# The output projection of a two-branch attention layer: eight block products, or seven with sums that DMAs make

## The chip, the cores and the metric

The kernel runs on one core of a Trainium2 chip. The metric is device time in microseconds, the median of several executions. TensorE (PE in the profile) multiplies, VectorE (DVE), ScalarE (ACT) and GpSimd (POOL) do the elementwise work, SyncE (SP) issues most DMAs. PSUM is the memory that TensorE writes to, SBUF the other on-chip memory.

## The reference

One layer on x of 1024 tokens by 1024, everything in float32:

```python
u = layer_norm(x) * (1 + scale) + shift          # scale, shift, gate = silu(c) @ w_ada + b_ada
fq, fk, fv, fg, ff, sq, sk, sv, sg = split(u @ w_in)
f_cum = cumsum(log_sigmoid(ff + b_f))
y_fox = softmax(causal(fq fk^T / 8 + f_cum_q - f_cum_k)) fv * silu(fg)     # 8 heads of 64
y_sb  = stick_breaking(sq, sk) sv * silu(sg)                               # 8 heads of 64
y = concat(y_fox, y_sb) @ w_out
out = layer_norm(2 ** 0.25 * x + gate * y, ln_g, ln_b)
```

The change is in the last two lines. Both are done tile by tile of 128 tokens.

## The kernel before

**Precision.** A float32 factor is split in a rounded part hi and a remainder lo, and a product is three TensorE products: hi·hi, lo·hi and hi·lo. One such group of three, 128 tokens by 128 of k by 512 columns, is called a step below.

**Stages.** The start makes scale, shift and the normalised u. Then the eight pairs of heads p = 0..7 follow (0 to 3 stick-breaking, 4 to 7 softmax). The attention of a pair is cut into 16 units (p, h, i): head h, block of 128 queries i. A unit has scores S on TensorE, softmax or stick-breaking on DVE, ScalarE and GpSimd, transposes T two units later, and for every two blocks a product with v ("pv"), from which `att_pv` makes a y piece of 64 x 256: ScalarE copy, DVE sum of the parts, GpSimd product with the gate branch (`sg`), and a DMA to the DRAM tensor `y_dr`. Between the units TensorE does "fillers": projections of the next pairs. In the last pair, from unit LAST + 4 on (LAST = 112 is its first), the fillers are steps of the output projection, in the numbers of TAIL: 68 steps before the loop ends, 60 after it.

**The order.** TensorE runs in the order in which the code is written, by hand (`manual_schedule`). The other engines get their order from a scheduler with modelled times. Every engine runs its own list in order: an instruction that waits holds all behind it.

**The output projection.** `gen_split_out`, beside the fillers of pairs 4 to 6, loads w_out in half blocks of 128 x 512, multiplies them by gate, and splits them on GpSimd into hi and lo, which go to DRAM (`wo_dr`). `load_wo` fetches them back in the last pair. `load_y` fetches y for a tile of 128 tokens and splits it on GpSimd. For pair 7, y does not go through DRAM: it stays in SBUF as `y7h` and `y7l`. `gen_out` makes 8 token tiles x 2 halves of 512 columns x 8 pairs = 128 steps, in the order of tiles 6, 7, 4, 5, 2, 3, 0, 1.

**The ending of a tile** (`o_half`, `ln_finish`), on DVE: 2^0.25 x + accumulator (L897), statistics (L899), aggregate (L170), GpSimd's two small operations for 1 / sqrt(var + eps) (L175, L176), two operations with gain (L910) and two with bias (L912), and the store. `lngb` is ln_g and ln_b in SBUF, for the first tiles; after the last unit `ln_to_psum` copies them to PSUM (`ps_gain`, `ps_bias`), and the rest use these.

## Time and profile before

| | |
|---|---|
| median of three runs | 684.96 us (684.79 to 685.23) |
| span of the profiled execution | 683.5 us |
| granted TensorE clock | 0.999 |
| TensorE busy | 667.2 us, 98% of the span, 4021 products recorded |
| VectorE, ScalarE, GpSimd busy | 450.6, 382.0, 427.7 us |
| first step of the output projection | 570.28 us |
| last pv product | 628.53 us |
| last TensorE product begins | 676.37 us |
| last store issued | 680.74 us |

The span runs from the first instruction to the last of the one profiled execution; the time of a run has 1.5 us more. A row of the timeline reads: start, duration, engine, line, operation, out<-in, shape, and in brackets the idle time before it and what ended it. A row of groups has its count, busy time and mean in ns at the end. Where a row says x2, its duration is that of two neighbours together. A few of TensorE's records are missing in a trace.

### The profile page before, as it was taken

The page shows a single profiled execution, that of the slowest core. Times are in us where ns is not written, and L with a number is a line of the kernel's source. Part 1 is how long each engine was busy: PE and PEld are TensorE (multiplying, and loading weights), DVE is VectorE, ACT ScalarE, POOL GpSimd, SP SyncE. Part 2 cuts the span into 40 slices and gives each one's busy share as a digit, 9 for nine tenths or more (in the row PEclk, how much of TensorE's full clock was granted, in tenths as well). Part 3 has the DMA queues.
Part 4 walks back from the last instruction along what each step waited for, and adds up shares of the span by engine and source line. Part 5 has one row for each costly group of instructions (what it writes and reads, how often), then busy time and mean ns, then how long its engine had stood idle before and what let it go on. Part 6 is the DMA issues. An engine that isn't in the chain of part 4 may idle for free.

```text
span 683.5 us, 11770 instructions
## 1 busy us (share of the span) xinstructions
PE 667.2 (98%) x4021; PEld 587.2 (86%) x4021; DVE 450.6 (66%) x914; ACT 382.0 (56%) x861; POOL 427.7 (63%) x558
## 2 busy tenths in 40 slices
PE   5999999999999999999999999999999999999995
PEld 4789898888998888889988888899988889888885
DVE  6785368867666667676675665765566677774645
ACT  5668357856567666566675564655565667531000
POOL 5558977756348566556388896877584364665411
PEclk9999999999999999999999999999999999999999
DMA  9966231112102121122144563453341298143301
GB/s 338 410 236 233 82 105 44 41 29 60 29 9 86 27 57 54 37 55 55 55 131 136 172 176 121 143 166 129 101 150 40 72 327 318 58 162 118 123 31 62
DMA packets 45036, 81.60 MB, mean 119 GB/s; under 512 B 5232, under 2 KB 18864, under 8 KB 44976
## 3 DMA queue, kind: packets, MB, share of 16 engines
q1 hardware_dynamic: 43536, 76.63, 33.8%
q10 hardware_dynamic: 1440, 4.21, 2.2%
q8 instruction: 32, 0.52, 0.3%
q14 instruction: 28, 0.23, 0.1%
HBM read 60.34 MB, written 16.29 MB: 112 GB/s over the span
## 4 chain that ended last, share of the span: by engine, by line
PE 94%; DMA 3%; DVE 2%; ACT 0%; issue 0%; POOL 0%; DVEq 0%
PE m L270 10%; PE m L272 10%; PE m L271 10%; PE pv L493 10%; PE T L478 9%; PE S L428 5%; PE S L427 5%; PE o L884 4%; PE o L882 4%; PE o L883 4%; PE v L327 4%; PE v L328 4%; PE v L329 4%; DMA raws<-in_w_qkg_dram 2%; PE st_late L589 1%; PE st_q L589 1%
## 5 line engine op out<-in xcount | busy, mean ns | idle before, releaser
L270 PE MATMUL m<-uh,whi 128*128 128x512 f32 x304 | 126.4, 416 | 0.0
L272 PE MATMUL m<-uh,wlo 128*128 128x512 f32 x304 | 119.7, 394 | 0.0
L271 PE MATMUL m<-ul,whi 128*128 128x512 f32 x304 | 119.7, 394 | 0.0
L481 DVE TENSOR_TENSOR pt<-T,pt 128x512 fp32r<-128x512 f32 (+2 forms) x192 | 100.5, 550 | 17.5 <-ACT pt L480 16.5
L461 POOL TENSOR_TENSOR be<-be,kp 128x127 f32<-128x127 f32 (+3 forms) x64 | 77.2, 1207 | 33.1 <-DVE kp L457 23.5
L480 ACT CAST pt<-T 128x512 fp32r<-128x512 f32 (+2 forms) x192 | 85.8, 480 | 16.1 <-PE T L478 12.5
L453 DVE TENSOR_TENSOR_SCAN kp<-kp,floor 128x512 f32<-128x512 f32 (+2 forms) x64 | 65.2, 1018 | 31.2 <-ACT kp L447 30.1
L493 PEld LDWEIGHTS pv<-pt,v 128*128 128x128 f32 (+1 forms) x640 | 77.1, 163 | 4.4 <-DVE pt L481 0.7
L493 PE MATMUL pv<-pt,v 128*128 128x256 f32 (+3 forms) x640 | 80.4, 271 | 0.5 <-DVE pt L481 0.5
L442 POOL TENSOR_SCALAR a<-a,l 128x1024 f32<-128x1024 f32 (+3 forms) x64 | 48.1, 751 | 40.3 <-DVE l L441 26.7
L272 PEld LDWEIGHTS m<-uh,wlo 128*128 128x128 f32 x304 | 57.1, 188 | 13.6
L440 ACT ACTIVATE a<-a,nm 128x1024 f32<-128x1024 f32 (+3 forms) x64 | 49.8, 778 | 33.8 <-DVE nm L434 32.7
L427 PE MATMUL S<-k,q 128*128 128x512 f32 (+5 forms) x192 | 66.5, 348 | 0.2 <-DVE nm L434 0.2
L428 PE MATMUL S<-kl,qz 128*128 128x512 f32 (+5 forms) x192 | 65.5, 342 | 0.0
L270 PEld LDWEIGHTS m<-uh,whi 128*128 128x128 f32 x304 | 57.3, 188 | 8.5 <-DVE kl L258 0.2
L271 PEld LDWEIGHTS m<-ul,whi 128*128 128x128 f32 x304 | 57.4, 189 | 8.0
L434 DVE CUSTOM_DVE_ANT_0 a<-S,fb 128x1024 f32<-128x1024 f32 (+3 forms) x64 | 48.3, 755 | 20.1 <-PE S L428 9.3
L514 POOL TENSOR_TENSOR ty<-ty,sg 64x256 f32<-64x256 f32 x64 | 47.5, 742 | 22.3 <-DVE ty L513 11.1
L447 ACT ACTIVATE kp<-S 128x128 f32<-128x128 f32 (+3 forms) x64 | 41.7, 652 | 31.6 <-PE S L428 29.4
L327 PE MATMUL v<-whi_v,uh 128*128 128x256 f32 (+1 forms) x192 | 56.0, 292 | 0.0
L405 ACT CAST qz<-q 64x128 fp32r<-64x128 f32 x128 | 37.4, 295 | 33.2 <-PE S L428 31.8
L328 PE MATMUL v<-whi_v,ul 128*128 128x256 f32 (+1 forms) x192 | 54.2, 282 | 0.0
(285 smaller groups left out, 1593.6 us busy)
## 6 DMA issues: line engine op xcount, KB each, us to landing
raw<-in_w_qkg_dram SPq DMA_DIRECT2D x38, 256.0 KB, 2.9
wss<-in_w_ss_dram SPq DMA_DIRECT2D x16, 512.0 KB, 8.4
x<-in_x_dram SPq DMA_DIRECT2D x8, 512.0 KB, 6.9
k<-k SPq DMA_DIRECT2D x32, 128.0 KB, 2.3
wg<-in_w_gate_dram SPq DMA_DIRECT2D x8, 512.0 KB, 4.9
raw_o<-in_w_out_dram SPq DMA_DIRECT2D x16, 256.0 KB, 2.8
fb<-f_dr ACTq DMA_DIRECT2D x8, 512.0 KB, 4.3
wo_dr<-whi_o SPq DMA_DIRECT2D x16, 256.0 KB, 2.5
```

Source lines behind the costliest of these rows:

```text
L270: nc.tensor.matmul(acc, hi[:, c], u_hi[kt][:, s], start=(kt == 0), stop=False)
L271: nc.tensor.matmul(acc, hi[:, c], u_lo[kt][:, s], start=False, stop=False)
L272: nc.tensor.matmul(acc, lo[:, c], u_hi[kt][:, s], start=False, stop=(kt == NB - 1))
L327: nc.tensor.matmul(acc[:, :n], u_hi[kt][:, ts_], hi[:, s], start=(kt == 0), stop=False)
L328: nc.tensor.matmul(acc[:, :n], u_lo[kt][:, ts_], hi[:, s], start=False, stop=False)
L427: nc.tensor.matmul(S[:, s, :w], qst[p][h][:, qs], kst[p][h][:, ks], start=True, stop=False)
L428: nc.tensor.matmul(S[:, s, :w], z, klo[p][:, ks], start=False, stop=True)
L453: scan = nc.vector.tensor_tensor_scan(rv, rv, floor[0][:, 512 - n:][:, ::-1], initial=0.0, op0=ALU.mult, op1=ALU.max)
L461: nc.gpsimd.tensor_tensor(be[:, :ke - 1], be[:, :ke - 1], kp[:, 1:ke], op=ALU.mult)
L480: nc.scalar.copy(hi[:, :n, qo:qo + P], t3)
L481: nc.vector.tensor_tensor(lo[:, :n, qo:qo + P], t3, hi.bitcast(F32)[:, :n, qo:qo + P], op=ALU.subtract)
L493: nc.tensor.matmul(acc[:m, q0:256], vt[p][:, kb, h * P:h * P + m], pt[:, kb % 4, q0:], start=start, stop=stop)
```

## The change

Let A be y (tokens by k) cut into A11, A12 (tokens 0 to 511, k 0 to 511 and 512 to 1023) and A22 with A21 below, and B the gated w_out in the same four blocks. Seven products of sums replace the eight of blocks (Winograd's form of Strassen's scheme):

- P1 = A11·B11, P2 = A12·B21, P3 = S4·B22, P4 = A22·T4, P5 = S1·T1, P6 = S2·T2, P7 = S3·T3. S are sums of blocks of y, T of weight blocks.
- Each is 4 tiles of 128 tokens (t0 to t3) x 4 blocks of k x 3 products: 112 steps in place of 128. Lower tokens' rows (r_4 to r_7, tokens 512 to 1023) take P1, P7, P6, P4, P5; upper rows (r_0 to r_3) P1, P6, P5, P2, P3. TensorE's order is P1 and P7 (t0, t1, then t2, t3), P6, then P4 and P5 (t0, t1, then t2, t3), then P2 and P3 of t3, t2, t1, t0. The last, P3 of t0, is in two groups of 256 columns.
- All sums are additions: `evac_g` gives the gate branch a minus for tokens 0 to 511, and `gen_split_out` gives the gate a minus for columns 512 to 1023, later for all, so that y and weights are stored with the signs that the sums want.
- A copy from DRAM to DRAM (`copied`, on SyncE) and then a DMA that adds (`add_in`, on GpSimd's queue) make a sum. There are 14 of them: T1, T3, T2, T4 and S3 whole (1 MB), S1 and S2 together in three parts, S4 in three. `PREP` lists at which unit each is issued; the last part of S4 is issued after the loop, when the last y piece is in DRAM.
- Splits: B11, B21, B22 as before on GpSimd; T3, T4, T1 with hi on ScalarE, stored split; T2 and all y operands are split when loaded (`cast`: hi on ScalarE, lo on GpSimd, or on DVE for S3, S1, S4). Pair 7's y goes through DRAM like the others.
- Lower rows take x when the P7 is ready, and end with a normalisation on ScalarE (`lower_done`: sum, two squares, final scaling; small operations on GpSimd) and `lower_out` (x ln_g on GpSimd, + ln_b on DVE). Upper rows begin with `upper_start` (x and the sums of P1, P6 and P5; tiles 0 and 1 on GpSimd, 2 and 3 on DVE), and end as before (`upper_done`).
- Buffers are regrouped: `gate` shares a tag with a start buffer, `raw` has three buffers, nm and l share a tile, ty is half as wide. `fetch_w`'s splits stand behind the sixth-last weighting of GpSimd (`weighed`). From LAST + 8 on SyncE too keeps the written order.

```diff
+    START_ON_POOL = (0, 1)
+    LOW_ON = {"S3": nc.vector, "S1": nc.vector, "S4": nc.vector}
+    STAGED = ("B11", "B21", "B22", "T3", "T4", "T1")
...
     def evac_g(p, ch, acc, sg):
...
-        nc.scalar.activation(sg[:, s], acc, AF.Tanh, scale=0.5)
-        nc.vector.scalar_tensor_tensor(sg[:, s], sg[:, s], 1.0, acc, op0=ALU.add, op1=ALU.mult)
+        sign = 1.0 if ch else -1.0
+        nc.scalar.activation(sg[:, s], acc, AF.Tanh, scale=0.5 * sign)
+        nc.vector.scalar_tensor_tensor(sg[:, s], sg[:, s], sign, acc, op0=ALU.add, op1=ALU.mult)
...
-        if p == NPAIR - 1:
...
-            nc.scalar.copy(yh[r, qs], yt[r, :])
-            nc.gpsimd.tensor_tensor(yl[r, qs], yt[r, :], yh.bitcast(F32)[r, qs], op=ALU.subtract)
-        else:
-            nc.sync.dma_start(y_dr[p, r, qs], yt[r, :])
+        nc.sync.dma_start(y_dr[p, r, qs], yt[r, :])
...
+    def add_in(out, src):
+        nc.gpsimd.dma_start(out, src, accum_op=ALU.add, max_dma_last_dim=2048)
+
+    def copied(out, src):
+        nc.sync.dma_start(out, src)
+
+    def cast(hi, lo, raw, high=None, low=None):
+        if high is nc.gpsimd:
+            nc.gpsimd.tensor_scalar(hi, raw, 1.0, 1.0, op0=ALU.mult, op1=ALU.mult)
+        else:
+            nc.scalar.copy(hi, raw)
+        (low or nc.gpsimd).tensor_tensor(lo, raw, hi.bitcast(F32), op=ALU.subtract)
...
+            if n == 9:
+                add_in(b_dr["T1"], b_dr["B11"])
...
+        add_in(b_dr["T3"], b_dr["B22"])
+        add_in(b_dr["T2"], b_dr["T1"])
...
+            if n == 2:
+                add_in(b_dr["T4"], b_dr["T2"])
...
+    def sums_first():
+        copied(s_dr["S1"], y_dr[0:4, :, HIGH])
+        copied(s_dr["S3"], y_dr[0:4, :, HIGH])
+
+    def sums_third():
+        add_in(s_dr["S3"], y_dr[0:4, :, LOW])
+
+    def sums_copy():
+        copied(s_dr["S2"], s_dr["S3"])
+
+    def sums_low(a, b):
+        for n in ("S1", "S2"):
+            add_in(s_dr[n][a:b], y_dr[4 + a:4 + b, :, HIGH])
+
+    def sums_last(a, b):
+        copied(s_dr["S4"][a:b], s_dr["S2"][a:b])
+
+    def sums_high(a, b):
+        add_in(s_dr["S4"][a:b], y_dr[4 + a:4 + b, :, LOW])
...
+    def block_step(acc, yname, wname, t, j, a=0, b=512):
+        yh, yl = (v[:, t * P:(t + 1) * P] for v in yop[yname, j, "t"])
+        hi, lo = w_of(wname, j, a, b)
+        acc = acc[:, :b - a]
+        nc.tensor.matmul(acc, yh, hi, start=j == 0, stop=False)
+        nc.tensor.matmul(acc, yl, hi, start=False, stop=False)
+        nc.tensor.matmul(acc, yh, lo, start=False, stop=j == 3)
...
+    def lower_done(t):
...
+        nc.scalar.activation(r, r, AF.Identity, accum_out=sums[:, 0:1])
+        nc.gpsimd.tensor_scalar(mv[:, 0:1], sums[:, 0:1], -1.0 / D, 1.0, op0=ALU.mult, op1=ALU.mult)
+        for x_, s in enumerate((LOW, HIGH)):
+            nc.scalar.activation(squares[x_], r[:, s], AF.Square, bias=mv[:, 0:1],
+                                 accum_out=(sums[:, 1:2], mv[:, 1:2])[x_])
...
+        nc.scalar.activation(r, r, AF.Identity, scale=rs[:, 0:1], bias=rs[:, 1:2])
+
+    def lower_out(t):
+        r, row = lower[t], 4 + t
+        for s in (LOW, HIGH):
+            nc.gpsimd.tensor_tensor(r[:, s], r[:, s], lgb[0][0][:, s], op=ALU.mult)
+            nc.vector.tensor_tensor(r[:, s], r[:, s], lgb[0][1][:, s], op=ALU.add)
...
+    def upper_start(t):
...
+            if t in START_ON_POOL:
+                nc.gpsimd.tensor_scalar(r, r, ALPHA, 1.0, op0=ALU.mult, op1=ALU.mult)
+                nc.gpsimd.tensor_tensor(r, r, part, op=ALU.add)
+            else:
+                nc.vector.scalar_tensor_tensor(r, r, ALPHA, part, op0=ALU.mult, op1=ALU.add)
...
+    PREP = [(16 * 4 + 5, sums_first), (16 * 4 + 12, sums_third), (16 * 5 + 2, sums_copy),
...
+            (LAST + 12, last_low)]
...
+    sums_high(3, 4)
+    for j in (1, 2):
+        y_ring("S4", j)
```

Three places of the lists that the engines run in order. The first is GpSimd's list after the change, from the last y piece (`ty_7_1_0`) on; `mv`, `rs` and `sums` are the small values of a lower tile's normalisation, the DMA is the last addition into S4, `yA12_1_1` the low parts of A12's blocks 2 and 3:

```order
L520 TENSOR_TENSOR ty_7_1_0_7850<-ty_7_1_0_7850,sg_7_6881 64x256
L1037 TENSOR_SCALAR mv_4_7876<-sums_4_7872 128x1
L843 DMA s_S4_101<-y_dr_90 128x512
...
L853 TENSOR_TENSOR yA12_1_1_7841<-yA12_1_1_7841,yA12_1_0_7840 128x512
...
L1044 TENSOR_TENSOR rs_5_7887<-mv_5_7890,rs_5_7887 128x1
L1050 TENSOR_TENSOR r_4_7090<-r_4_7090,ln_g_7785 128x512 x2
L1050 TENSOR_TENSOR r_5_7178<-r_5_7178,ln_g_7785 128x512 x2
L853 TENSOR_TENSOR yA12_1_1_7841<-yA12_1_1_7841,yA12_1_0_7840 128x512
L1037 TENSOR_SCALAR mv_6_7984<-sums_6_7980 128x1
```

Rows 4 and 5 have their products with ln_g ahead of the low part of A12's fourth block.

The second is VectorE's list after the change, from the sums with P5 of t2 (`p5_2`) to those with P3 of t3 (`p3_3`); `wlo_S4_3` is the low part of S4's fourth block:

```order
L1051 TENSOR_TENSOR r_4_7090<-r_4_7090,ln_b_7786 128x512
L1061 SCALAR_TENSOR_TENSOR r_2_7931<-r_2_7931,c1_1_7534 128x512
L1061 SCALAR_TENSOR_TENSOR r_2_7931<-r_2_7931,u2_1_7677 128x512
L1051 TENSOR_TENSOR r_4_7090<-r_4_7090,ln_b_7786 128x512
...
L1051 TENSOR_TENSOR r_5_7178<-r_5_7178,ln_b_7786 128x512 x2
L1061 SCALAR_TENSOR_TENSOR r_3_7789<-r_3_7789,u2_1_7677 128x512
L1019 TENSOR_TENSOR r_3_7789<-r_3_7789,p2_3_8045 128x512
L1026 BN_STATS st_b3_8061<-r_3_7789 128x6
L853 TENSOR_TENSOR wlo_S4_3_7942<-wlo_S4_3_7942,whi_S4_3_7941 128x512
L1019 TENSOR_TENSOR r_3_7789<-r_3_7789,p3_3_0_8063 128x512
```

The rows' endings and the upper starts stand ahead of that low part. It is followed by the endings of four upper tiles and of lower rows 6 and 7.

The third is VectorE's list before, in the place that answers to it, the ending of a tile (`o_3` is the accumulator of token tile 3):

```order
L897 SCALAR_TENSOR_TENSOR r_3_7922<-xr_3_7920,o_3_0_7895 128x512
L899 BN_STATS st_b3_7923<-r_3_7922 128x6
L897 SCALAR_TENSOR_TENSOR r_3_7922<-xr_3_7920,o_3_1_7926 128x512
L899 BN_STATS st_b3_7923<-r_3_7922 128x6
L170 BN_AGGR mv_b3_7953<-st_b3_7923 128x2
L910 SCALAR_TENSOR_TENSOR r_3_7922<-r_3_7922,mv_b3_7953,ps_gain_7832 128x512 x2
L912 SCALAR_TENSOR_TENSOR r_3_7922<-r_3_7922,rs_b3_7955,ps_bias_0_7833 128x512
L912 SCALAR_TENSOR_TENSOR r_3_7922<-r_3_7922,rs_b3_7955,ps_bias_1_7834 128x512
```

VectorE's list there held only the tiles' endings, one tile after the other.

More of the change, by code (lines that the diff above doesn't have):

```diff
@@ new lines, in load_op @@
+    def load_op(name, jp, tags):
+        pair = wop[name, jp] = [big(tag, {"q": 4, "k": 4, "pth": 3, "ptl": 3}.get(tag, 1), f"w{name}_{jp}_{x_}", F32R)
+                                for x_, tag in enumerate(tags)]
+        if name in STAGED:
+            for x_, t in enumerate(pair):
+                nc.sync.dma_start(t.bitcast(F32), wo_dr[OPS.index(name), x_, jp])
+            return
+        for d in range(2):
+            hi, lo = (t[:, d * 512:d * 512 + 512] for t in pair)
+            nc.sync.dma_start(lo.bitcast(F32), b_dr[name][2 * jp + d])
+            cast(hi, lo, lo.bitcast(F32), low=LOW_ON.get(name))
@@ L835, in tile_hybrid_layer @@
     lgb = {}
     def load_ln():
-        lgb[0] = sb.tile([P, 2, D], F32, tag="v", bufs=3, name="lngb")
-        nc.sync.dma_start(lgb[0][:, 0, :], ln_g.to_broadcast([P, D]))
-        nc.sync.dma_start(lgb[0][:, 1, :], ln_b.to_broadcast([P, D]))
+        lgb[0] = [att_tile(f"ln_{x_}") for x_ in "gb"]
+        nc.sync.dma_start(lgb[0][0], ln_g.to_broadcast([P, D]))
+        nc.sync.dma_start(lgb[0][1], ln_b.to_broadcast([P, D]))
     ps_ln = []
@@ new lines, in tile_hybrid_layer, with y_src, y_split, y_big @@
+    yop = {}
+    SOURCE = {"A11": lambda j: y_dr[j, :, LOW], "A22": lambda j: y_dr[4 + j, :, HIGH],
+              "A12": lambda j: y_dr[4 + j, :, LOW]}
+    def y_src(name, j):
+        return SOURCE[name](j) if name in SOURCE else s_dr[name][j]
+    def y_split(name, j, pair):
+        hi, lo = yop[name, j, "t"] = pair
+        nc.sync.dma_start(lo.bitcast(F32), y_src(name, j))
+        cast(hi, lo, lo.bitcast(F32), low=LOW_ON.get(name))
+    def y_big(name, jp):
+        t = sb.tile([P, 2, 2, 512], F32R, tag="v", bufs=3, name=f"y{name}_{jp}")
+        for d in range(2):
+            y_split(name, 2 * jp + d, [t[:, d, x_, :] for x_ in range(2)])
@@ new lines, in tile_hybrid_layer, with load_rows, load_upper, add_to @@
+    lower, upper, c1, u2 = {}, {}, {}, []
+    def load_rows(t):
+        lower[t] = big("k" if t < 2 else "q", 4, f"r_{4 + t}")
+        nc.sync.dma_start(lower[t], x[(4 + t) * P:(5 + t) * P, :])
+    def load_upper(t):
+        upper[t] = att_tile(f"r_{t}")
+        nc.sync.dma_start(upper[t], x[t * P:(t + 1) * P, :])
+    def add_to(r, s, acc, op=ALU.add):
+        nc.vector.tensor_tensor(r[:, s], r[:, s], acc, op=op)
+    stats = {}
+    def row_stats(r, t, h, s, n=2):
+        if h == 0:
+            stats[t] = sb.tile([P, 3, 6], F32, tag="st", bufs=3, name=f"st_b{t}")[:, :n, :]
+        nc.vector.bn_stats(stats[t][:, h, :], r[:, s])
```

385 lines of the change are left out of this document (257 added, 128 removed).

## The prediction

> **What bounds the kernel now.** I read the page's busy shares first, then the chain that ended last, then TensorE's waits, then the busy time by stretches of the last 120 us, where the change has its work.
>
> ```profile
> PE 667.2 (98%) x4021; PEld 587.2 (86%) x4021; DVE 450.6 (66%) x914; ACT 382.0 (56%) x861; POOL 427.7 (63%) x558
> ...
> PE 94%; DMA 3%; DVE 2%; ACT 0%; issue 0%; POOL 0%; DVEq 0%
> ```
>
> ```profile
> PE sc_all L163 <- POOL later L313: 5.4, 1, 5.4
> ...
> PE S L427 <- DVE nm L434: 0.2, 1, 0.2
> ```
>
> ```profile
> 560.00:580.00 20.00, 20.00 (x132) 18.15 (x130) 14.43 (x35) 14.12 (x32) 9.65 (x11) 1.00 0.90 353
> 580.00:600.00 20.00, 20.00 (x120) 17.44 (x118) 16.06 (x42) 11.73 (x32) 12.37 (x17) 1.00 0.16 50
> 620.00:640.00 20.00, 20.00 (x90) 16.20 (x89) 12.62 (x20) 1.63 (x4) 10.02 (x13) 1.00 0.44 149
> 640.00:660.00 20.00, 20.00 (x88) 16.09 (x87) 10.14 (x17) 0.00 (x0) 6.58 (x10) 1.00 0.16 59
> ```
>
> TensorE holds 94% of the chain. Its one long wait is at the start; after 300 us it waits 0.2 us in all (the row of S). In the stretches the columns are the length, then busy time of PE, PEld, DVE, ACT and POOL, the granted clock, DMA share and GB/s. PE is full in every one, at clock 1.00, so a product taken out shortens the program as long as the operands stay in time and no other engine has more to do than PE. From 640 us on DVE has half of its time free, ScalarE all and GpSimd two thirds: there the new work must fit.
>
> ```profile
> L882 PE MATMUL o<-woh,y7h x4: 388/396/398, 631.0 to 647.8; 128*128 128x512 f32 x4
> ```
>
> ```profile
> 628.53 0.57 PE L493 MATMUL pv<-pt,v 128*128 128x256 f32 x4
> ...
> 630.48 0.74 POOL L514 TENSOR_TENSOR ty<-ty,sg 64x256 f32<-64x256 f32 x1
> ...
> 676.37 0.28 PE L884 MATMUL o<-wol,y7h 128*128 128x256 f32 x1
> 677.14 0.43 DVE L899 BATCH_NORM_STATS2 st_b<-r 128x6 f32<-128x256 f32 x1
> 680.74 0.41 SPq L921 DMA_DIRECT2D out_dram<-r  x1
> ```
>
> The first row gives the price of a step: four uses of pair 7, eight steps apart, 16.8 us for 24 steps, so 0.70 us a step of three products, 0.233 us a product. The last statistics end at 677.57, and what follows them (normalisation, the store that SyncE issues at 680.74) is the same afterwards. The last attention product (628.53) and the y piece made from it (630.48) stay where they are, since the same 68 steps stand ahead of them. The span ends at 683.5; the median, 684.96, lies 1.5 above it, and I add the sum to the median.
>
> **What is removed.** 128 steps become 112: 16 × 0.70 = **−11.2 us**, to 673.8. This needs all else to be hidden.
>
> **What is added to the other engines in the last stage.**
>
> ```profile
> L897 DVE SCALAR_TENSOR_TENSOR r<-xr,o 128x512 f32<-128x512 f32 x15 | 10.2, 686 | 22.6 <-PE o L884 22.5
> L899 DVE BATCH_NORM_STATS2 st_b<-r 128x6 f32<-128x512 f32 x15 | 10.4, 693 | 0.4
> L170 DVE BATCH_NORM_AGGREGATE mv_b<-st_b 128x2 f32<-128x12 f32 x7 | 1.4, 206 | 0.2
> 644.78 1.40 DVE L910 SCALAR_TENSOR_TENSOR r<-r,mv_b,ps_gain 128x512 f32<-128x512 f32 x2
> ```
>
> ```profile
> L126 POOL TENSOR_TENSOR wlo<-raw,whi 128x512 fp32r<-128x512 f32 x38 | 49.1, 1297 | 2.4 <-DMA wo_dr<-wlo_o 0.8
> 644.83 0.22 POOL L175 TENSOR_SCALAR rs_b<-mv_b 128x1 f32<-128x1 f32 x1 [0.37 <-DVE mv_b L170]
> 645.14 0.57 POOL L176 TENSOR_TENSOR rs_b<-rs_b,mhalf 128x1 f32<-128x1 f32 x1
> ```
>
> ```profile
> L440 ACT ACTIVATE a<-a,nm 128x1024 f32<-128x1024 f32 x8 | 9.2, 1152 | 6.4 <-DVE nm L434 6.4
> L440 ACT ACTIVATION_READ_ACCUMULATOR a<-a,nm 128x1 f32 x64 | 12.0, 187 | 0.0
> L480 ACT CAST pt<-T 128x512 fp32r<-128x512 f32 x60 | 34.3, 587 | 4.8 <-PE T L478 3.2
> ...
> y_dr<-ty SPq DMA_DIRECT2D x56, 64.0 KB, 1.9
> ```
>
> *Deadlines.* Without a stall the pace of 0.70 us puts the product of P2 t3 that needs A12's fourth low part at 645.2, and that of P3 t3 that needs S4's fourth low part at 648.0; from the end of P3 t3 PE has 24 steps, 16.8 us.
>
> *The chain to A12's fourth low part.* The last y piece ends on GpSimd at 630.48 + 0.74 = 631.2; mv_4 (0.22) follows. The squares of row tile 4, two casts of S4 and A12, the sum of tile 5, two more casts and the squares of tile 5 then run on ScalarE in order: four squares at 0.587 + 0.187, four casts at 0.587, one sum at 1.152 + 0.187, 6.8 us, to 638.3. GpSimd waits with tile 5's four small operations (0.22 + 0.22 + 0.57 + 0.22, with gaps 1.4), to 639.7. The issue of the addition into S4 stands on GpSimd ahead of this and waits for y to land (631.2 + 1.9, after the store's issue); no row prices an accumulating DMA's issue, and 0.4 (SyncE's issue at 680.74) to 2.0 us (the landing of 64 KB) both fit into the time that ScalarE takes: 0. Then, in GpSimd's order, come four products with ln_g, 1.30 each, and only then the low part, 1.30: 646.2. So P2 t3 is late by 1.0 at the least.
>
> *The chain to S4's fourth low part.* It stands on DVE behind 11 operations that begin with row 4's ln_b addition, each 0.69 to 0.72. It ends near 650.0, 0.8 after it is needed, if nothing lengthens them.
>
> *DVE's last list.* From P3 t3's end to the last statistics DVE has 22 single 512-wide operations at 0.72 (686 or 693 ns and the gap), three pairs at 1.33, four 256-wide at 0.46 (0.43 and the gap), three aggregates at 0.24: 15.8 + 4.0 + 1.8 + 0.7 = 22.4 us. PE has 16.8, and 0.9 follow its end before (676.65 to 677.57). So DVE ends 22.4 − 17.7 = **4.7 us** later than PE's pace lets it; this is a bound by DVE that even punctual operands do not lift.
>
> **What the two engines do to each other.** Before, DVE's second tensor came mostly from PSUM. Now ln_b additions, upper starts, and low parts of S1, S3 and S4 read two SBUF tensors on DVE: 32 operations of the kind, with GpSimd reading SBUF beside them.
>
> ```profile
> L412 DVE TENSOR_TENSOR fb<-fb,ps_causal x63: 269/286/290, 350.1 to 604.7; 128x128 f32<-128x128 f32 x63
> L412 DVE TENSOR_TENSOR fb<-fb,causal x1: 1106/1106/1106, 346.5 to 346.5; 128x128 f32<-128x128 f32 x1
> 346.13 1.32 POOL L126 TENSOR_TENSOR wlo_o<-raw_o,whi_o 128x512 fp32r<-128x512 f32 x1
> ...
> 632.88 1.29 POOL L863 TENSOR_TENSOR wlo_y<-yr,whi_y 128x512 fp32r<-128x512 f32 x1
> 633.62 1.76 DVE L910 SCALAR_TENSOR_TENSOR r<-r,mv_b,lngb 128x512 f32<-128x512 f32 x2
> 634.26 0.54 POOL L175 TENSOR_SCALAR rs_b<-mv_b 128x1 f32<-128x1 f32 x1
> ```
>
> The mask addition takes 286 ns with its mask in PSUM and 1106 with both in SBUF, and that one began at 346.5 inside the GpSimd operation of 346.13 to 347.45, and ended just after it. The pair at 633.62 takes 1.76 and not 1.40, GpSimd's scalar beside it 0.54 and not 0.22. So such operations take turns. The Trainium skill states this ("SBUF — State Buffer", Who interferes with whom): a VectorE instruction with two SBUF inputs and a GpSimd instruction that reads SBUF exclude each other, the one that issues first holding the port to its end. By that rule the sum is the one below; were the pair at 633.62 the whole price (0.36 a pair), the two terms would shrink to 1.4 and 1.2 and the time to some 682.
>
> Turn by turn: GpSimd's ln_g product, DVE's ln_b addition or upper start, and again. Three DVE operations of 0.69 to 0.72 go between the four products and the low part, which ends at 648.3 to 648.5 and not 646.2. P2 t3 is late by **3.3 us** (bounds 1.0, no meeting, and 4.8, two more turns at 0.72) and ends near 649.0. DVE has eight of its 11 operations left at 648.3; they end at 653.9, the low part at 654.6, or near 655.5 with one meeting with GpSimd's starts of r_1 and products of r_6. P3 t3, from 649.0 on, needs it at 651.3: **4.2 us** (bounds 0.8 and 5.5, one more 1.30).
>
> **ScalarE and DVE in the stretch 560 to 600.** Low y was split on GpSimd before; now ten casts of S3, A11 and T2 (0.587 each, 5.9 us) stand on ScalarE among the exponentials, and S3's low parts on DVE. ScalarE's 14.12 of 20 becomes 20. PE has steps of the projection to fill with, but scores and transposes stand in written order: nothing to 4 us (5.9 less what 580:600 has free of ScalarE, less queueing that I cannot see); I take **1.0**, nearer nothing, since the transposes run two units behind the scores.
>
> **The weight sums, splits and DMAs of the attention.** GpSimd splits 12 half blocks of weights where it split 16, and takes 12 low parts of T3, T4 and T1 besides: 12 × 1.30 less four splits of one to two such operations each, 5 to 10 us more, over three pairs of heads in which PE hides it as it hid the rest (0.2 us of waits): **0**, with its upper bound under the third rival.
>
> **Sum**: 684.96 − 11.2 + 1.0 + 3.3 + 4.2 + 4.7 = **687.0 us**, slower by 2.0. From the other end: the last statistics at 655.5 + 0.5 + 22.4 = 678.4, and 1.0, where they ended at 677.6.
>
> **The rivals.**
>
> *First: the two engines hardly meet, faster.* GpSimd's products fall into DVE's operations on PSUM; then the late terms are 1.0 and 0.8: 684.96 − 11.2 + 1.0 + 1.0 + 0.8 + 4.7 = 681.3. For it: before, the eight subtractions with an SBUF gain mostly took little more than the 0.70 us of each with a PSUM gain (the pair at 644.78), as the median of this row shows; against it, GpSimd was half idle there (10.02 of 20) and now has a row of five long operations.
>
> ```profile
> L910 DVE SCALAR_TENSOR_TENSOR r<-r,mv_b,lngb x8: 739/770/1106, 596.2 to 634.6; 128x512 f32<-128x512 f32 x8
> ```
>
> If DVE moreover gets through a third of its 4.7 us ahead, and ScalarE's term is nothing, 678.5. This case decides wherever the two late terms together stay below 4.1, by which the sum comes to 683.6.
>
> *Second: all hidden*, 673.8. It asks that DVE does 22.4 us of work in 17.7.
>
> *Third: GpSimd held up by its own DMAs.* Each of 14 additions stands in GpSimd's order and waits for the DMA that wrote its source; T4's waits for T2's to land, 1 MB. The nearest row lands 512 KB in 7.7 us:
>
> ```profile
> wol<-wo_dr SPq DMA_DIRECT2D x8, 512.0 KB, 7.7
> ```
>
> so up to 15 us less some 4 us of GpSimd operations that stand between the two (an estimate: two parts of splits, two weightings, a y piece), with weights of softmax queued behind that PE's transposes need. If half of that reaches PE, 5 to 6 us: 687.0 + 6 = 693. Against it: that time is one of a burst; 256 KB lone take 2 to 3. The Trainium skill says ("SBUF — State Buffer", A bandwidth-pool intuition that's wrong (but worth ruling out)) that such a DMA can take about 3100 ns beside VectorE's copies that takes 620 alone; an estimate by that page is 2.5 us more for each of the additions, of which those with a waiter count. No run shows a GpSimd DMA yet.
>
> **How the numbers follow.** A measurement here tells 0.2% from no change: 683.6 to 686.3. The main case, with its three open terms half-way to their bounds, lies at 683.6 to 689.9 and has 0.47, of which 0.12 lies under 686.3. The first rival, 677 to 683.6, has 0.40: the rows show the turn-taking itself, but how often the engines meet is a matter of tenths of a microsecond. The third, 690 to 698, has 0.10, all hidden 0.03. So faster 0.43 (0.40 + 0.03), same 0.12, slower 0.45 (0.35 + 0.10). The range, 679 to 693, leaves out the early end of the first rival, all hidden and the upper half of the third.
>
> **What would show it.** In the changed profile: PE's busy time lower by 11; TensorE waits of some 3 us at P2 t3 for A12's low part and of some 4 at P3 t3 for S4's; ln_g products on GpSimd over 1.4 us, or ln_b additions over 0.9; DVE without a gap in the last 22 us, with the last statistics after 678. I am wrong if PE waits for neither part, if the last statistics come before 675, or if PE waits in the attention for a softmax weight behind a GpSimd DMA.

## The result and the profile after

The changed kernel takes 720.76 us (715.46 to 723.63) where the kernel before takes 684.97: a ratio of 1.051 (95% interval 1.049 to 1.053). It is slower, as forecast, but by 36 us and not by 2, well outside the range of 679 to 693.

The page of the changed kernel: busy times, the DMA queues, the chain that ended last by engine.

```profile
span 721.9 us, 11956 instructions
...
PE 670.0 (93%) x3961; PEld 585.6 (81%) x3961; DVE 468.3 (65%) x934; ACT 419.5 (58%) x929; POOL 462.2 (64%) x586
...
q1 hardware_dynamic: 50608, 103.90, 42.5%
q0 software_dynamic: 4320, 8.39, 7.1%
...
PE 66%; DMA 13%; DVE 7%; POOL 6%; issue 5%; ACT 2%; SPq 1%; POOLq 0%; DVEq 0%; ACTq 0%
```

The chain is 66% TensorE where it was 94%; DMA has 13%. q0 is the queue of GpSimd's DMAs, and 8.39 MB are the fourteen additions.

*Where* the time goes is read from one VectorE instruction that starts every softmax unit (out `a`, from the scores). Its start in the first unit of the last pair, before and after:

```profile
552.79 1.23 DVE L434 CUSTOM_DVE_ANT_0 a<-S,fb 128x1024 f32<-128x1024 f32 x1 [1.25 <-PE S L428]
```

```profile
584.93 1.22 DVE L443 CUSTOM_DVE_ANT_0 a<-S,fb 128x1024 f32<-128x1024 f32 x1 [1.34 <-PE S L437]
```

It is 32.1 us late. The same row is 1.6 late at the first unit of the first softmax pair (350.45 for 348.85) and 33.8 late at the last unit (646.49 for 612.72); the span is 38.4 longer (the profiled execution took 723.63 us). So some 30 of the 38 us are lost between 390 and 580 us, in the attention, 1.6 in the last pair, 4.6 behind its last scores.

*What* TensorE waits for there (waits: the waiting instruction, the one it waited for, us in all, times, longest):

```profile
PE T L487 <- POOL a L451: 15.9, 5, 7.7
...
PE S L436 <- DVE nl L443: 4.7, 2, 3.7
PE p L1005 <- POOL yA L853: 2.9, 1, 2.9
...
PE pv L500 <- ACT pt L489: 2.4, 1, 2.4
```

The first row is new: transposes wait for the softmax weights `a` that GpSimd scales. GpSimd and SyncE in the longest of these waits:

```profile
383.16 1.30 POOL L843 DMA_DIRECT2D s_S<-y_dr  x1 [5.77 <-DMA s_S<-y_dr]
...
399.04 1.10 POOL L843 DMA_DIRECT2D b_T<-b_B  x1 [6.75 <-DMA b_T<-raw_oB]
399.81 1.84 POOL L451 TENSOR_SCALAR a<-a,nl 128x128 f32<-128x128 f32 x2
```

```profile
388.47 0.60 SPq L875 DMA_DIRECT2D wo_dr<-whi_oB  x1
398.33 0.48 SPq L846 DMA_DIRECT2D s_S<-s_S  x1
...
399.53 0.38 SPq L129 DMA_DIRECT2D raw<-in_w_qkg_dram  x1
```

GpSimd stands 6.75 us with the addition into T1 (399.04) at the head of its list; the addition waits for a 256 KB store that SyncE issued at 387.09, and two rows of weights `a` are behind it. That store took 11.4 us to land, where its sixteen take 3.1 in the median; it moved beside the addition into S3. SyncE stands from 389 to 398.33 with the copy of S3 into S2, which waits for the addition into S3 issued at 383.16. TensorE stands 7.66 us, and then goes slowly for a while (windows: length, busy PE, PEld, DVE, ACT, POOL, granted clock, DMA share, GB/s):

```profile
393.00:401.00 8.00, 0.39 (x2) 0.39 (x3) 0.28 (x2) 0.96 (x2) 1.96 (x3) 0.72 0.90 261
401.00:404.00 3.00, 3.00 (x11) 2.44 (x11) 0.29 (x1) 0.64 (x2) 1.33 (x2) 0.60 0.25 91
404.00:408.00 4.00, 4.00 (x25) 3.47 (x24) 2.70 (x6) 2.13 (x6) 0.62 (x1) 1.00 1.11 253
```

From 401 to 404 it starts 11 products in 3 us, from 404 to 408 25 in 4 us. So the stop costs more than its length: the unit is 9.2 us late after a wait of 7.66.

The second large stop has another look: the addition into T2 stands behind the addition into T3 with no awaited DMA in its row.

```profile
477.82 1.04 POOL L843 DMA_DIRECT2D b_T<-b_B  x1
...
488.45 1.07 POOL L843 DMA_DIRECT2D b_T<-b_T  x1 [8.93 <-DVE v L345]
```

The addition into T2 was issued 0.3 us after the one into T3 had landed (488.13).

The landing times are the size that the prediction lacked: an addition of 1 MB into T takes 9.0 to 13.3 us from issue to landing, the one into S3 15.2, those of 512 KB 8.9 to 12.1, those of 256 KB 4.3 to 9.3.

### The profile page after: what moved, and what is told of

It reads as the page before. It is cut to its first block, busy times and chain, and to the rows that moved or that the text cites. A ratio compares the mean times of both kernels' runs of the same rounds, so it can differ in the third digit from the quotient of the medians.

```text
span 721.9 us, 11956 instructions
## 1 busy us (share of the span) xinstructions
PE 670.0 (93%) x3961; PEld 585.6 (81%) x3961; DVE 468.3 (65%) x934; ACT 419.5 (58%) x929; POOL 462.2 (64%) x586
## 3 DMA queue, kind: packets, MB, share of 16 engines
q0 software_dynamic: 4320, 8.39, 7.1%
## 4 chain that ended last, share of the span: by engine, by line
PE 66%; DMA 13%; DVE 7%; POOL 6%; issue 5%; ACT 2%; SPq 1%; POOLq 0%; DVEq 0%; ACTq 0%
PE pv L500 7%; PE T L487 7%; PE m L279 7%; PE m L280 7%; PE m L281 7%; PE v L336 3%; PE S L436 3%; PE v L337 3%; PE v L338 3%; PE S L437 3%; DMA b_T<-raw_oB 2%; DMA raw_oT<-b_T 2%; DMA s_S<-y_dr 2%; PE p L1004 2%; DMA r<-in_x_dram 1%
## 5 line engine op out<-in xcount | busy, mean ns | idle before, releaser
L451 POOL TENSOR_SCALAR a<-a,nl 128x1024 f32<-128x1024 f32 (+3 forms) x64 | 53.1, 853 | 22.7 <-DVE nl L450 14.7
L449 ACT ACTIVATE a<-a,nl 128x1024 f32<-128x1024 f32 (+3 forms) x64 | 49.8, 778 | 29.1 <-DVE nl L443 25.6
L443 DVE CUSTOM_DVE_ANT_0 a<-S,fb 128x1024 f32<-128x1024 f32 (+3 forms) x64 | 48.3, 755 | 22.3 <-PE S L437 11.8
L487 PE MATMUL T<-ident,a 128*128 128x128 f32 x288 | 44.3, 282 | 17.8 <-POOL a L451 15.9
L520 POOL TENSOR_TENSOR ty<-ty,sg 64x256 f32<-64x256 f32 x64 | 49.0, 766 | 17.5 <-DVE ty L519 8.7
```

What stands on the lines that cost most here:

```text
L487: nc.tensor.transpose(tp[:, b * P:(b + 1) * P], a[:, kb * P:(kb + 1) * P], ident)
```

## The experiments

Every time stands against 685 us for the kernel before, run on the same chip beside it.

**Which part costs what.** Five kernels leave parts out.

```diff
 def add_in(out, src):                      # no sums
-    nc.gpsimd.dma_start(out, src, accum_op=ALU.add, max_dma_last_dim=2048)
+    return
 def copied(out, src):
-    nc.sync.dma_start(out, src)
+    return
```

> All 14 additions and all DRAM-to-DRAM copies are left out; S operands are read straight from blocks of y, T operands from blocks of the weights, so every load, split, product and ending stays but the result is not the layer's. Theory A (engines that run in order wait for DMAs whose landing the additions and copies have stretched to 9 to 15 us, so that TensorE waits for softmax weights): the stalls of the attention, 30 us in all, go, and only the last stage's own losses of the prediction stay: 684 to 690 us. Rival B (the engines' own added work and the turn-taking of VectorE and GpSimd cause the stalls): 705 us or more.

Measured 693.96 us (1.0129, 1.0106 to 1.0153). The additions and copies cost 26.8 of the 36 us.

The T additions alone left out (the four `add_in(b_dr["T..."], ...)`), and the y sums alone left out:

> Only the four additions of weight sums (T1, T3, T2, T4) are left out; the y sums stay. Theory A: the two longest stalls, +9.2 us at pair 4 and +6.5 at pair 5 against before, go, and a part of the later ones: 700 to 707 us. Rival B: 716 us or more. Rival C (the copies of y, 2 MB at 371 us, are what stretches the landings): the stall at pair 4 stays, so 712 to 716 us.

> All sums of y (10 additions, 5 copies) are left out, S operands read blocks of y; the four additions of weights stay. The fourth corner beside after (720.8), no T additions (708.7) and no sums (694.0). If the two groups cost independently: 694 + 12 = 704 to 708 us. If they stretch one another's landings: under 702 us, since one group alone then costs less than its share.

Measured 708.65 (1.035, 1.0329 to 1.0371) and 700.27 (1.022, 1.0205 to 1.0235). So the T additions by themselves cost 6.3, the y sums by themselves 14.7, both 26.8: 5.8 more than their sum.

On top of the kernel without sums, the second split of T3, T4 and T1 left out, the ending of the lower rows left out, and both:

```diff
-        order_ = [(name, j) for name in STAGED if name[0] == "T" for j in range(4)]
+        order_ = []                         # no second split; B22, B21, B11 are loaded in place of T3, T4, T1
...
         for s in (LOW, HIGH):               # no ending of the lower rows
-            nc.gpsimd.tensor_tensor(r[:, s], r[:, s], lgb[0][0][:, s], op=ALU.mult)
-            nc.vector.tensor_tensor(r[:, s], r[:, s], lgb[0][1][:, s], op=ALU.add)
```

> As the kernel without sums, and the second splitting of T3, T4 and T1 (12 loads, 12 splits, 24 stores) is left out; T operands read splits of plain blocks. If ScalarE's waits for these loads, at the head of its list in pair 6, cost TensorE the 5.5 us that the trace without sums loses there: 687 to 690 us. If the loss there has another cause: 692 us or more.

> As the kernel without sums, and the lower rows are stored without ln_g and ln_b: eight GpSimd products and eight VectorE additions are left out. By the prediction's terms (turns 2.3 and 3.4, and four of the additions in VectorE's last list, 2.9): 684 to 688 us. If only the turn-taking of the additions counted, which moving ln_b to PSUM already took out (1.3 us): 691.5 to 693 us.

> The kernel without sums and without the second splitting of T (688.6 us), and the lower rows are stored without ln_g and ln_b. If the costs are independent: 688.6 - 4.6 = 684 us, so that seven products with everything of theirs free still only reach the kernel before. If the last stage's waits hang on the transfers of the splits: 681 us or less.

Measured 688.58 (1.005, 1.0035 to 1.0065), 689.4 (1.0057, 1.0038 to 1.0075) and 687.42 (1.0032, 1.0021 to 1.0042). The split costs 5.4, the ending 4.6, both 6.5, less than their sum. With sums, split and ending free of charge the seven products are still 2.4 us slower than the eight: TensorE still waits there for sums on VectorE (1.26 and 1.61 us) and for a cast of S4 (3.13).

**VectorE's second SBUF operand.** The ln_b addition of the lower rows reads its bias from PSUM, in the kernel without sums:

```diff
-            nc.vector.tensor_tensor(r[:, s], r[:, s], lgb[0][1][:, s], op=ALU.add)
+            nc.vector.tensor_tensor(r[:, s], r[:, s], ps_ln[1][s.start // 512], op=ALU.add)
```

> As the first kernel of this set (no sums), and the eight additions of ln_b to lower rows read ln_b from PSUM in place of SBUF, so that they are no longer operations with two SBUF inputs. If VectorE and GpSimd take turns as the prediction says, these eight no longer take part: 1.5 to 4 us less than without this edit. If turn-taking costs nothing here: within 0.7 us of it.

Measured 692.65 (1.0111, 1.0095 to 1.0126): 1.3 us. The eight rows of the line without and with the edit (count, minimum, median, maximum in ns):

```profile
L1051 DVE TENSOR_TENSOR r<-r,ln_b x8: 672/682/1765, 650.3 to 682.8; 128x512 f32<-128x512 f32 x8
```

```profile
L1051 DVE TENSOR_TENSOR r<-r,ps_bias x8: 669/680/691, 648.9 to 680.1; 128x512 f32<-128x512 f32 x8
```

The long ones are gone, the rest is as it was: the engines do take turns, but the median of the eight shows that most do not meet.

**Is it the place of the additions in the lists?** All additions and copies held behind the GpSimd weighting that stands last at their place; the additions into T1, T2, T4 and S3 and the copy into S2 moved later, and T1 split ahead of T4:

```diff
-        nc.gpsimd.dma_start(out, src, accum_op=ALU.add, max_dma_last_dim=2048)
+        with after(*weighed[-1:]):
+            nc.gpsimd.dma_start(out, src, accum_op=ALU.add, max_dma_last_dim=2048)
...
-            if n == 9:
+            if n == 12:
...
-    PREP = [(16 * 4 + 5, sums_first), (16 * 4 + 12, sums_third), (16 * 5 + 2, sums_copy),
+    PREP = [(16 * 4 + 5, sums_first), (16 * 4 + 15, sums_third), (16 * 5 + 8, sums_copy),
```

> All sums are made, but each addition and copy is put behind the latest weighting of GpSimd at the point where it is written, and the first ones are written some units later, so that GpSimd and SyncE reach them when their sources should have landed. The bytes are the same. Theory A in the form that a wait at the head of GpSimd's list is the cost: 698 to 708 us, with no wait of GpSimd over 3 us for an addition. If the traffic alone stretches the landings of weights and splits (raw loads), whoever waits: 714 us or more.

Measured 730.57 (1.0661, 1.0643 to 1.0679), 10 us worse. The delay at the end of the first softmax pair is smaller, 6.7 us where it had been 14.1; in the seventh pair it grows from 9.9 to 39.2 us. GpSimd no longer stands at the additions into S3 and T1; other stops come later, on SyncE and ScalarE too.

**Is it the wait for data?** In the kernel without sums, fourteen additions of the same sizes from a part of w_out into DRAM tensors that nobody reads, with no data awaited:

```diff
+        n = out.shape[0]
+        with after(*weighed[-1:]):
+            nc.gpsimd.dma_start(scratch.pop(0)[:n], w_out[:n * P, LOW].rearrange("(a p) n -> a p n", a=n),
+                                accum_op=ALU.add, max_dma_last_dim=2048)
```

> As the kernel without sums, with 14 accumulating DMAs of the same sizes put back at about their units on GpSimd's queue, but from a part of w_out into scratch tensors that nobody reads: no instruction waits for what they write, and they wait for no source (the copies stay out). What is left is their issue on GpSimd and their traffic. If the waits for sources and sums make the cost (W): within 3 us of the kernel without sums, 693 to 697 us. If the traffic alone stretches the other loads and writes until engines wait for those (T): 704 us or more, half of the 26.8 us between that kernel and the changed one.

Measured 727.53 (1.0607, 1.0556 to 1.0658). Additions that wait for nothing and that nobody waits for cost as much, so the theory of data waits alone fell. GpSimd's list shows why here:

```profile
411.10 1.22 POOL L846 DMA_DIRECT2D z<-in_w_out_dram  x1
...
419.61 0.37 POOL L452 TENSOR_SCALAR a<-a,nl 128x128 f32<-128x128 f32 x1
427.21 1.09 POOL L846 DMA_DIRECT2D z<-in_w_out_dram  x1 [7.23 <-issue]
```

The second addition of 1 MB stood 7.23 us with nothing awaited ("issue"), until the first, issued 16 us before, had landed (15.85 us after its issue). A second stop of this kind is longer:

```profile
504.16 1.04 POOL L846 DMA_DIRECT2D z<-in_w_out_dram  x1 [10.78 <-DVE fb L422]
```

It too ends 0.3 us after the addition ahead has landed (503.84); the instruction named has nothing to do with it. These stops are not the whole cost. Of the 36 us by which this run's last scores are late, 6 arise in the sixth pair, behind the first stop, and 27 in the seventh. There ScalarE also stands 6.04 us for a load of y that waits for no addition: issued at 520.50, beside an addition of 1 MB, it took 10.2 us to land, where the two of its place took 5.1 and 5.4 without sums. So additions seem to delay other transfers as well, and this run does not tell the two costs apart.

**Is it the adding?** `accum_op` dropped, so that the same DMAs copy, on the same queue, at the same places, with the same waits:

```diff
-        nc.gpsimd.dma_start(out, src, accum_op=ALU.add, max_dma_last_dim=2048)
+        nc.gpsimd.dma_start(out, src, max_dma_last_dim=2048)
```

> The 14 accumulating DMAs become plain copies of the same bytes from the same queue, with the same waits and places; the sums are wrong by that. If the adding itself makes these DMAs slow and holds the DMA engines (D1): their landings fall from a median near 9 us to 5 or 6, the waits behind them shrink, and the time falls to 702 to 710 us. If any DRAM-to-DRAM transfer of these sizes at these places costs this (D2): 716 to 724 us.

Measured 705.08 (1.0287, 1.0257 to 1.0317): the adding costs 15.7 of the 26.8 us; the fourteen DMAs as copies, with the copies of SyncE, 11.1. The queue of GpSimd's DMAs in this run, and the additions of T3 and T2, 1.3 us apart:

```profile
q0 software_dynamic: 2272, 8.39, 3.7%
```

```profile
473.41 0.69 POOL L843 DMA_DIRECT2D b_T<-b_B  x1
...
474.69 0.69 POOL L843 DMA_DIRECT2D b_T<-b_T  x1
```

The same bytes took 2272 packets, not 4320, and mostly landed sooner (in the median of T1 and T3 8.2 us where the additions took 11.8, of T2 and T4 7.3 where they took 9.4; S3 8.7, not 15.2; 256 KB into S 4.8, not 6.4; but T2, now issued right behind T3, 9.5, not 9.0). An issue occupied GpSimd 0.58 to 0.69 us in the median, not 0.92 to 1.07.

**Room for descriptors.** The theory from these rows (R in the expectations): an addition of 1 MB fills the space that GpSimd's DMA descriptors have, and the next one stops GpSimd until it has drained. The space was doubled in the kernel with unawaited additions and in the changed kernel; SBUF was full, so a raw weight tile went for it.

```diff
-        return sb.tile([P, 528], F32, tag="wraw", bufs=3, name=name)
+        return sb.tile([P, 528], F32, tag="wraw", bufs=2, name=name)
...
-    nc = _bacc.Bacc("TRN2", target_bir_lowering=False, num_devices=1, dynamic_dma_scratch_size=2048)
+    nc = _bacc.Bacc("TRN2", target_bir_lowering=False, num_devices=1, dynamic_dma_scratch_size=4096)
```

> The kernel of 727.53 us (no sum used; fourteen accumulating DMAs of the same sizes into scratch tensors that nobody reads, without waits for data) with 4096 instead of 2048 bytes per partition reserved for the descriptors of GpSimd's DMAs, and, to make room, two instead of three buffers for the raw weight tiles. Theory R (room for descriptors): GpSimd stood still without any awaited instruction at 420 to 427 and at 493 to 504 us because the descriptors of a 1 MB addition filled the space and the next addition could not be written until that one had drained. With twice the space both stops (7.2 and 10.8 us of idle time) go, and the time falls to 700 to 715 us. Rival, traffic: the additions' bytes and packets delay the loads and stores of the list by themselves, whatever the space; then the stops stay or move and the time is 724 to 731 us.

> The changed kernel whole, with the same two edits: 4096 instead of 2048 bytes for the descriptors, two instead of three raw tiles. Theory R: the 8.93 and 3.92 us that GpSimd stood between the additions of T3, T2 and T4 go, and with them most of the products' delay there (6.45 us between the second units of the sixth pair); the stop at 393 us, which is a wait for a store that landed 11.4 us after its issue, stays. About 708 to 716 us. Rival, traffic: 718 to 724 us. If the third raw tile was what the list needed, it is above 724 us.

> The changed kernel with two instead of three raw weight tiles and the room for descriptors as it was. It is the control for the run of 744.63 us, which had both edits. Theory R: the room was worth some 8 us, so this is about 750 to 758 us. Rival, traffic: the room is worth nothing, 742 to 747 us. If the third raw tile costs nothing, about 721 us, and then the wider room itself did harm.

Measured 739.98 (1.0801, 1.078 to 1.0822) and 744.63 (1.086, 1.0837 to 1.0883), and the control of the second, the raw tile gone and the space as before, 743.99 (1.0852, 1.0826 to 1.0877); the first has no control. So the raw tile is worth 23 us here, and the space nothing measurable, in a kernel that then waits for its raw tiles; with three tiles the space could not be tried. The rows of the additions into T2 and T4, in the wider space and in the control:

```profile
499.85 1.40 POOL L843 DMA_DIRECT2D b_T<-b_T  x1
...
516.34 1.07 POOL L843 DMA_DIRECT2D b_T<-b_T  x1 [9.69 <-DMA b_T<-b_T]
```

```profile
507.05 1.03 POOL L843 DMA_DIRECT2D b_T<-b_T  x1 [9.40 <-issue]
...
516.78 1.07 POOL L843 DMA_DIRECT2D b_T<-b_T  x1 [4.48 <-DMA wo_dr<-wlo_oB]
```

In the wider space the additions of T3 and T2 were issued 0.7 us apart (499.14 and 499.85), in the control 10.4: the stop for room had gone. But the addition into T4, which reads T2, then stood 9.69 us until T2 had landed, 16.1 us after its issue. So of 13.9 us of standing 9.7 stayed, as a wait for data.

The stop was then measured by itself, in the kernel without sums and second split: DMAs into tensors that nobody reads, back to back, where the DMA engines have little else.

```diff
+    def probe(count, n, **how):
+        for _ in range(count):
+            with after(*weighed[-1:]):
+                nc.gpsimd.dma_start(scratch.pop(0)[:n], w_out[:n * P, LOW].rearrange("(a p) n -> a p n", a=n),
+                                    max_dma_last_dim=2048, **how)
```

> The kernel of 688.58 us (no sums, no second split) with eleven DMAs of GpSimd's into scratch tensors that nobody reads, issued back to back with nothing awaited, in the second to fourth pair, where the DMA engines are 10 to 20% busy: two accumulating ones of 1 MB, two plain ones of 1 MB, three accumulating ones of 512 KB, four accumulating ones of 256 KB. Theory R (room for descriptors, one 1 MB addition fills it): GpSimd stops before the second 1 MB addition, and the instruction behind waits about as long as the first takes to land, 5 to 10 us; the two plain ones, with half the packets, go out within 2 us; of the three of 512 KB two go out within 2 us and the third waits; the four of 256 KB go out one after the other, 1 us apart. Rival, traffic: with nothing else moving, all go out about 1 us apart, and GpSimd stops nowhere.

The four places, in the order of that text (an "x2" is that many neighbours in one row):

```profile
160.04 1.29 POOL L1221 DMA_DIRECT2D z<-in_w_out_dram  x1
170.08 1.06 POOL L1221 DMA_DIRECT2D z<-in_w_out_dram  x1 [8.74 <-issue]
...
218.36 1.38 POOL L1221 DMA_DIRECT2D z<-in_w_out_dram  x2
...
261.24 2.84 POOL L1221 DMA_DIRECT2D z<-in_w_out_dram  x3
...
305.04 3.35 POOL L1221 DMA_DIRECT2D z<-in_w_out_dram  x4
```

Two additions of 1 MB: a stop of 8.74 us, nothing awaited, in quiet traffic; the second went out 0.3 us after the first had landed (169.81). Two plain copies of 1 MB: none. Four additions of 256 KB: none. This is theory R's forecast, but for the third of 512 KB, which should have stood and did not; so a plain count of bytes in flight is not the rule. It took 695.37 us, in one execution; the first softmax unit was 4.8 us later than without the probes, for one stop of 8.74.

**Without that stop.** The four T additions as sixteen of 256 KB, one row block each, spread over the list:

```diff
-                add_in(b_dr["T1"], b_dr["B11"])
+                parts(*PIECES.get(n, ""))
...
+        PIECES = {9: ("T10",), 10: ("T11",), 11: ("T12",), 12: ("T13", "T30"), 13: ("T20",), 14: ("T31",), 15: ("T21",)}
+        LATER = {0: ("T33", "T40"), 1: ("T23", "T41"), 2: ("T42",), 3: ("T43",)}
```

> The changed kernel with the four additions of 1 MB of the T sums as sixteen of 256 KB, each a row block, spread over the list's steps. Same bytes, same packets, twelve issues more at GpSimd (about 11 us of its time). Theory R: GpSimd stops for room no more (8.9 and 3.9 us between the additions of T3, T2 and T4), and no long wait for one store stands ahead of an addition: 706 to 716 us. Rival, traffic: 718 to 726 us.

Measured 724.57 (1.0577, 1.0559 to 1.0595), 4 us worse. The stop between T3 and T2 is gone (the sixth pair, where it cost 6.5 us, ends with the delay it began with), but the delay grows by 10.5 us in the fifth pair and by 23 in the seventh, where it had been 12.5 and 10. SyncE and GpSimd at the first of these stops:

```profile
388.01 0.42 SPq L885 DMA_DIRECT2D wo_dr<-whi_oB  x1
396.80 0.48 SPq L846 DMA_DIRECT2D s_S<-s_S  x1
...
399.47 0.56 SPq L129 DMA_DIRECT2D raw<-in_w_qkg_dram  x1
```

```profile
393.16 1.05 POOL L520 TENSOR_TENSOR ty<-ty,sg 64x256 f32<-64x256 f32 x1
404.25 0.62 POOL L134 TENSOR_SCALAR whi<-raw 128x512 fp32r<-128x512 f32 x1 [10.04 <-DMA raw<-in_w_qkg_dram]
```

SyncE stands 8.4 us at the copy of S3 into S2, the raw weights behind it come late, and GpSimd stands 10 us at their split. In the seventh pair ScalarE stands up to 11.1 us at a T operand whose load SyncE could not issue:

```profile
ACT whi_oT L852 <- DMA raw_oT<-b_T: 23.4, 5, 11.1
```

**Without the copies' waits.** Later places for the copies (with the T additions in pieces); copies from y's own tensor (one into S2, three into S4), which wait for no addition, in the changed kernel; and the same with the T additions in pieces:

```diff
-        copied(s_dr["S2"], s_dr["S3"])
+        copied(s_dr["S2"], y_dr[0:4, :, HIGH])
...
-        copied(s_dr["S4"][a:b], s_dr["S2"][a:b])
+        copied(s_dr["S4"][a:b], y_dr[a:b, :, HIGH])
```

> The kernel of 724.57 us (T sums in sixteen pieces) with every copy of a sum held behind the GpSimd instruction that stands last in the list at its place, the copy of S3 into S2 four units later, the first copy into S4 three and the additions to it four units later. Theory H (a copy at the head of SyncE's list waits for a slow addition, and the raw tiles behind it come late): the stops of 10 us at 394 and 515 us go, 700 to 710 us. Rival, traffic: 718 to 726 us.

> The changed kernel with the five copies between sums taken from y's own tensor (S2 from the low channels of y's right half, S4 from the same) in place of S3 and S2, so that none waits for an addition and they go out early; the bytes are the same, the fourteen additions as they are. S2 and S4 lack a term each. Theory H: the stop at 393 us (SyncE stood 9.8 us at the copy) and those of the seventh pair shrink, 703 to 712 us, with GpSimd's own stops left. Rival, traffic: 717 to 723 us.

> Both: the T sums in sixteen pieces and the five copies from y's own tensor. S2 and S4 lack a term each. Theory H: neither GpSimd nor SyncE stands at a full queue or at a copy, so only the waits for the T sums' loads remain, 694 to 704 us (the kernel without sums took 693.96). Rival, traffic: 715 to 724 us, since every byte of the sums still moves.

Measured 722.5 (1.0555, 1.0533 to 1.0577), 717.27 (1.0469, 1.0446 to 1.0492) and 720.37 (1.0512, 1.048 to 1.0545). Theory H's 694 to 712 fell in all three. The delay at the first softmax pair's end shrinks (14.1 us in the changed kernel, 7.1 and 7.4 in the last two), and comes back in the seventh pair. There, in the last kernel, SyncE stands from 506.8 to 515.4 with the load of a T operand at its head, ScalarE behind it for 10.8 us:

```profile
506.30 0.45 SPq L521 DMA_DIRECT2D y_dr<-ty  x1
515.43 1.59 SPq L839 DMA_DIRECT2D raw_oT<-b_T  x2
```

**What is settled and what is open.** Settled: the additions and copies cost 27 us, 24 of them in the attention, and 16 because the DMAs add. The delay comes at stops of lists, of which three kinds were seen: GpSimd at an addition that cannot be issued, GpSimd at one whose source has not landed, and SyncE or ScalarE at a copy or load that waits for an addition. The first was taken away by the pieces, the second, at S3 and T1, by later places, the copies' part of the third by copies from y; each time, with three raw tiles, the total stayed between 717 and 731 us, with other stops in the trace. No run took away all three; additions with no waits for data gave 727.53. Open is how the 27 us divide: no run had all the bytes of the additions and none of the stops, so what the traffic alone would cost, and whether some order of the lists hides it, was not shown. Nor did a run make the sums without the second split, whose loads and stores stand in SyncE's list with the copies. The DMA engines' share between 350 and some 580 us rises with every part, by windows of the kernel before, without sums, with plain copies, and changed:

```profile
350.00:550.00 200.00, 199.74 (x1234) 177.01 (x1233) 125.68 (x332) 115.65 (x285) 144.02 (x164) 1.00 0.41 127
```

```profile
350.00:556.00 206.00, 200.33 (x1239) 177.07 (x1237) 125.36 (x329) 123.26 (x300) 150.89 (x166) 1.00 0.57 181
```

```profile
350.00:568.00 218.00, 207.35 (x1247) 181.79 (x1245) 127.24 (x334) 124.93 (x304) 156.70 (x176) 0.98 0.69 222
```

```profile
350.00:582.00 232.00, 208.90 (x1248) 183.78 (x1247) 127.36 (x334) 125.22 (x302) 159.87 (x175) 0.96 0.72 208
```

0.41, 0.57, 0.69 and 0.72. That this uses up the slack between a transfer's issue and its use is a reading that fits the late store and load above; no run shows it by itself. No version tried beats the kernel before.

## Why the prediction was right and wrong

- **The attention at 0: wrong, and the whole miss.** "The weight sums, splits and DMAs of the attention" stood with 0 because TensorE waits 0.2 us there before. From the first softmax unit to the last pair's first one the delay grows by 30.5 us in the changed kernel, by 6.2 without the sums, by 0.1 without the second split of T3, T4 and T1 (12 loads, 24 stores) too: some 24 for the sums, 6 for the split. The inference that failed is from a kernel with no waits to one whose lists have new instructions with waits at their heads: TensorE's 0.2 us showed that nothing was late, not how much could be late. The prediction's own sign of being wrong came: TensorE waits in the attention for softmax weights behind a GpSimd DMA (7.66 us at 400.62). "Slower" came true mostly by this term, which the sum had at nothing.
- **The third rival: the right mechanism at a fifth of its size.** It had GpSimd held up by its DMAs, 6 us, from one pair of additions (T2, T4) and the landing of 512 KB in 7.7 us. That pair stood 3.9 us. It left out T1's addition and S3's chain on two lists (9.2 and 3.1 us of delay), the stop from T3 to T2 (8.9), which no awaited DMA explains, and all stops on SyncE and ScalarE. That "256 KB lone take 2 to 3" spoke against it; those of 256 KB took 4.3 to 9.3 us as additions. Whether VectorE's copies lengthen these DMAs, the prediction's other price for them, no run separates.
- **The stops' price.** A wait was taken at its length. At 393 us it was 7.66 and the delay 9.2, since products start at half their rate for some 3 us after it. The Trainium skill ("TensorE: Matmul & The Clock Gate", Part 1: The HAM clock gate) says that TensorE, once it has idled for some 3.4 us, runs its first 3.4 us or so at half its clock. The trace agrees at this stop (a granted clock of 0.60 from 401 to 404); behind the stops of 4.00 us (490.63) and 3.67 (558.42) the clock stayed at 0.50 for longer, 4.9 and 5.4 us, and behind those of 3.17 (414.91) and 2.35 (524.49) it was 1.00.
- **P2 t3, forecast 3.3 us late by A12's low part: right.** The wait is 2.93. GpSimd's four products with ln_g stood ahead of it as said:

```profile
679.82 1.29 POOL L1050 TENSOR_TENSOR r<-r,ln_g 128x512 f32<-128x512 f32 x1
...
682.32 2.94 POOL L1050 TENSOR_TENSOR r<-r,ln_g 128x512 f32<-128x512 f32 x2
...
684.17 1.64 DVE L1061 SCALAR_TENSOR_TENSOR r<-r,c 128x512 f32<-128x512 f32 x1 [1.26 <-DMA r<-in_x_dram]
...
685.23 1.71 POOL L853 TENSOR_TENSOR yA<-yA,yA 128x512 fp32r<-128x512 f32 x1
685.74 1.75 DVE L1061 SCALAR_TENSOR_TENSOR r<-r,u 128x512 f32<-128x512 f32 x1
686.90 0.63 POOL L1037 TENSOR_SCALAR mv<-sums 128x1 f32<-128x1 f32 x1
```

  VectorE's upper starts take 1.64 and 1.75 us where they lie beside GpSimd's, 0.68 where GpSimd has one-column operations only (690.42): the turn-taking of the prediction, and the rule of the Trainium skill cited there, are borne out. The low part ends at 686.94, 16.2 us after the last y piece (670.76), against 17.1 to 17.3 forecast.
- **P3 t3, forecast 4.2 late by S4's low part:** TensorE waited 1.13 us there, and not for that part; with the granted clock of 690 to 695 (0.65 of 5 us, 1.75 lost) it is some 3 us late. That lies within the bounds, but from other causes. The part itself ends at 693.27, just ahead of its product at 693.66; at full clock TensorE would have needed it near 691.7 (an estimate: 689.33, three steps of 0.70 and a product), so the slow clock hid a wait for it.
- **VectorE's last list, 4.7 us over TensorE's pace: right in kind, 1 us too large.** TensorE's last product ends at 711.05, the last statistics at 715.63 (0.42 from 715.21), 4.6 later, where 0.9 lay between them before: 3.7.
- **The stretch 560 to 600 at 1.0: near.** The last pair, in which it lies, adds 1.6 us, and 0.7 in the kernel without sums.
- **From the last scores to the end** the sum made −11.2 + 3.3 + 4.2 + 4.7 = +1.0; it is +4.6. Missing are two waits that no step had, for a sum on VectorE at 657.79 (2.33 us) and for a cast of A12 (0.95), and the clock, 0.50 from 687.0 to 693.5, behind the wait at P2 t3. With the attention at 0, this end and the last pair's 1.6 would give some 691, inside the range. The kernel without sums and second split, which has the attention that the prediction assumed, took 688.58, 1.6 over the forecast. That is near by luck in part: TensorE waits there for S4's cast and low part (1.9 and 2.5 us, for the 4.2 of the sum), but for no low part of A12 (forecast 3.3), and VectorE's last list costs 1.7 and not 4.7.
- **PE's busy time lower by 11: not seen.** It is 670.0 where it was 667.2, since products at half clock are counted longer; without sums and split it is 659.6.

## What to carry to other kernels

A trace with no waits says nothing of how much lateness it can take: before an instruction with a wait is put into an in-order list, bound its landing by the largest row, add the clock lost behind the stop, and do so for every list it passes, SyncE's among them. Price a DMA that adds as a kind of its own, not as a copy. When a stop is taken away and the time stays, read which list stands next; here later places, pieces and copies without waits moved the stops, and the total by anything from 10 us up to 3.5 us down.
